# Two groups of a gated feed-forward as seven half-size products

## The chip, the core and the metric

The program runs on one core of a Trainium2 chip. The metric is the device time of one execution in microseconds (us). The three timed runs of the kernel before gave 1691.04, 1692.81 and 1693.84 us, so the median is 1692.81 us.

The engines are named as in the profile: PE (TensorE, matrix products; PEld is its weight load), DVE (VectorE), ACT (ScalarE), POOL (GpSimd), SP (SyncE, which here issues the loads of weights). All work in fp32: a product is made of three passes over operands that are split into a high part in the PE's own format (fp32r) and the rest (low part).

## The reference, cut to what matters

A decoder block of two layers is followed by a second block. The part that the change touches is that block's gated feed-forward: 512 tokens, model width 1024, inner width 2816.

```python
h = rmsnorm(x, g_ffn[i])
gate = causal_dwconv3(h @ w_gate[i], ffn_conv_w[i], ffn_conv_b[i])
x = x + (jax.nn.silu(gate) * (h @ w_up[i])) @ w_down[i]
```

`causal_dwconv3` adds to each token, per inner channel, weighted values of the two tokens before it. The gate's product and its partner's product (`h @ w_up`) have the same left operand.

## The kernel before

The normed tokens stand turned (features on partitions) as eight pairs of high and low parts, `xth` and `xtl`, 128 features by 512 tokens each. The inner width is cut into eleven groups (`gr`) of 256 channels. Each group has a part for the gate (`gp` in the profile) and one for the partner (`up`). `pair_of` loads the group's weights in two chunks of four feature blocks by 256 channels (`wr`, L170, 512 KB each). `split` makes the high part on ACT (`wh`, L119) and the low part on DVE (`wl`, L120). `mm3` issues three matmuls (L202 to L204) for each feature block and each half of the channels, with the weights stationary and all 512 tokens moving. So a part is 48 matmuls of 512 columns and a group is 96, accumulated in two PSUM banks per part.

`gate_ev` turns the gate's banks into `y`: a scaled copy on ACT (L1321), two DVE instructions for the convolution (L1322, L1324), then the silu on ACT (L1593). `up_ev` multiplies `y` by the partner's bank on DVE into `hr` (L1603). Group 0 is `gated_first`: its weights are there ahead, and it works on halves of 256 tokens, so that it can start when two of the four token tiles are normed and turned (`rms_norm`, L488 to L490, and `put_t`, L447). Groups 1 to 3 follow, then two rounds of `down_steps`. A round multiplies 1024 inner channels by `w_down` as seven products of half size: DVE makes sums of weight quarters (`wq`, L924) and of `hr` quarters (L915), `split` makes their parts (`wl`, `aop`), PE multiplies into banks `r`, and L885 adds them into `x`. Between the products of a round stand the parts of groups 4 to 10.

The order of the instructions on each engine is set at build time by a scheduler that takes the program's order and priorities (`high_priority`), and is fixed then; each engine works through its own list in order. Tiles come from pools: a new tile in a full pool waits until the old tile in its place has been read for the last time. The pool `wp` holds four pairs of `wh` and `wl`. The pool `fb` with the quarters of `w_down` opens after group 3 and takes memory that earlier pools have given back.

Of the kernel before, what the change touches and what calls it, by code (L numbers as in the profile page):

```python
# [12 lines left out]
F32 = mybir.dt.float32  # L13
F32R = mybir.dt.float32r
AF = mybir.ActivationFunctionType
ALU = mybir.AluOpType
AX = mybir.AxisListType

P = 128
# [7 lines left out]
W_PRIO = 60  # L27
# [17 lines left out]

WEAVE = (-1, -1, -1, 0, -1, 1, -1, -1, 2, -1, 3)
A_PRIO, B_PRIO = 120, 80
MLA_WO_AT = (0, 0, 21, 23)


@with_exitstack
def tile_hybrid_decoder(ctx: ExitStack, tc: tile.TileContext, io: dict, out: bass.AP):
    nc = tc.nc

    cst = ctx.enter_context(tc.tile_pool(name="cst", bufs=1))
    wp = ctx.enter_context(tc.tile_pool(name="wp", bufs=4))
# [6 lines left out]
    def pool(name, bufs, side=None):  # L63
        return tc.tile_pool(name=name, bufs=bufs, side=side, reuse_waits="tile")

    n_big = [0]

    def big(name, dt=F32R):
        n_big[0] += 1
        return bp.tile([P, 4, S], dt, tag="b", name=f"{name}_{n_big[0]}")  # L70

    def bank(name="pb"):
        n_big[0] += 1
        return ps.tile([P, S], F32, tag="ps", name=f"{name}_{n_big[0]}")
# [24 lines left out]
    def tick(n=1):  # L99

        clock[0] += 1
        while n and later and later[0][0] < clock[0]:
            later.popleft()[2]()
            n -= 1
# [13 lines left out]
    def split(hi, lo, src, src2=None):  # L118
        turned["hi"] = nc.scalar.copy(out=hi, in_=src).ins  # L119
        return nc.vector.tensor_tensor(out=lo, in0=src, in1=hi.bitcast(F32), op=ALU.subtract)  # L120
# [79 lines left out]
    def mm3(o, st, mv, start, stop):  # L200
        (sh, sl), (mh, ml) = st, mv
        nc.tensor.matmul(o, lhsT=sh, rhs=mh, start=start, stop=False, skip_group_check=True)  # L202
        nc.tensor.matmul(o, lhsT=sh, rhs=ml, start=False, stop=False, skip_group_check=True)  # L203
        nc.tensor.matmul(o, lhsT=sl, rhs=mh, start=False, stop=stop, skip_group_check=True)  # L204
# [43 lines left out]
    def krows(W, k0, kn, c0, n):  # L248
        return W[k0 * P:(k0 + kn) * P, c0:c0 + n].rearrange("(k p) c -> p k c", p=P)
# [316 lines left out]
    xt = new_xt()  # L566
# [22 lines left out]
    with ExitStack() as mla:  # L589
# [14 lines left out]
        def tmp(name):  # L604
            n_big[0] += 1
            return m4.tile([P, S], F32, tag="s", name=f"{name}_{n_big[0]}")
# [84 lines left out]
        for k in range(3):  # L691
            wh, wl = wchunk([(lambda raw: raw[:, :512].rearrange("p (h d) -> p h d", h=8),
                              w_uq[k * P:(k + 1) * P, :, 128:192])], 1, 512)
            rch.append((k, 1, wh, wl))
        for t in range(NB):
# [3 lines left out]
            a, b = tmp("ra"), tmp("rb")  # L699
# [3 lines left out]
            with tc.issue_after(turned["c"]):  # L703
                nc.vector.tensor_tensor(out=av, in0=pv, in1=rope[:, 0, t:t + 1, :].to_broadcast([P, 8, 64]),
                                        op=ALU.mult)
                nc.vector.tensor_tensor(out=bv, in0=pv, in1=rope[:, 1, t:t + 1, :].to_broadcast([P, 8, 64]),
                                        op=ALU.mult)
# [8 lines left out]
        PT, U = {}, {}  # L716
# [55 lines left out]
        for u in range(8 * NB + LAG + 1):  # L772
            h, qb = divmod(u, NB)
# [117 lines left out]
    ts2 = slice(0, 256), slice(256, 512)  # L891
# [185 lines left out]
    g, b = load_gb("ln_mix_g", "ln_mix_b", 0)  # L1077
    xt = new_xt()
# [67 lines left out]
    with swa:  # L1146
# [5 lines left out]
        PT, U, PO = {}, {}, {}  # L1152
# [162 lines left out]
    xt = new_xt()  # L1315
# [244 lines left out]
    xt = new_xt()  # L1560
# [11 lines left out]
    with pool("ff", 2) as ff:  # L1572
# [15 lines left out]
        def gate_ev(gr, banks):  # L1588
            for m in range(2):
                n_big[0] += 1  # L1590
                Y[gr, m] = y = ff.tile([P, S], F32, tag="y", name=f"y_{n_big[0]}")
                conv3(y, banks[m], V_FW, 22, gr * 2 + m, V_FB)
                nc.scalar.activation(y, y, AF.Silu)  # L1593

        def up_ev(gr, banks):
            if gr < 8 and gr % 2 == 0:
                RAW[gr // 2] = big("hr", F32)
            elif gr % 2 == 0:
                hh, hl = big("ah"), big("al")
                H.extend((hh[:, m, :], hl[:, m, :]) for m in range(4 if gr < 10 else 2))  # L1600
            for m in range(2):
                if gr < 8:
                    turned["y", gr] = nc.vector.tensor_tensor(  # L1603
                        out=RAW[gr // 2][:, gr % 2 * 2 + m, :], in0=Y.pop((gr, m)), in1=banks[m], op=ALU.mult).ins
                    continue
                n_big[0] += 1
                a = ff.tile([P, S], F32, tag="a", name=f"a_{n_big[0]}")
                nc.vector.tensor_tensor(out=a, in0=Y.pop((gr, m)), in1=banks[m], op=ALU.mult)
                split(*H[gr * 2 + m - 16], a)

        def gated(gr, part):

            banks = [bank("gu"[part] + "p") for _ in range(2)]
            pair_of(gr, (wg, wu)[part], banks)
            (gate_ev, up_ev)[part](gr, banks)

        def gated_first():
            banks = [bank("gt") for _ in range(2)] + [bank("up") for _ in range(2)]
            for hf in range(2):
                need(("xt", 2 * hf), ("xt", 2 * hf + 1))  # L1620
                for m in range(4):
                    half_m(banks[m], ahead.chunks[m], X, hf)
                    if hf == 0 and m < 2:
                        need(("xt", 2 + m))
            ahead.done()
            gate_ev(0, banks[:2])
            up_ev(0, banks[2:])
# [22 lines left out]
                to_ple(t)  # L1650

        gated_first()
        for gr in range(1, 4):
            for part in range(2):
                gated(gr, part)
        with pool("fb", 4) as fb:
# [108 lines left out]
```

## Time and profile before

| | |
|---|---|
| timed, median of 3 (range) | 1692.81 us (1691.04 to 1693.84) |
| the profiled execution | 1690.43 us, of which the profile spans 1688.6 us |
| busy: PE, DVE, ACT | 99%, 66%, 49% of the span |
| granted TensorE clock | 1.00 over the span |
| group 0 to the start of group 1 | 1270.81 to 1296.64 us |
| groups 1 to 3 | 1296.64 to 1361.94 us |

A matmul's time in the profile is from its start to its result, and the next one starts before that. What a matmul costs in a row of matmuls is therefore the distance between two starts. For DVE and ACT the time of one instruction is nearly what it costs.

### The profile page before, as it was taken

How to read it: one execution, taken by the hardware profiler on the slowest of the kernel's cores; microseconds unless marked ns; L12 is line 12 of the kernel's file. 1: busy time of each engine (PE TensorE's matmuls, PEld its weight loads, DVE VectorE, ACT ScalarE, POOL GpSimd, SP SyncE). 2: the span in 40 equal slices, each digit the busy share in tenths (PEclk: the TensorE clock that was granted, in tenths of full speed). 3: DMA queues.
4: the chain of work that ended last, by engine and by line, in shares of the span. 5: the costliest groups of instructions: out<-in, count | busy, mean ns of one | idle time of the engine just before them, and what ended most of it. 6: DMA issues, size and time to landing. Idle time of an engine off the chain costs nothing.

```text
span 1688.6 us, 21336 instructions
## 1 busy us (share of the span) xinstructions
PE 1669.5 (99%) x8239; PEld 1384.7 (82%) x8239; DVE 1111.0 (66%) x1938; ACT 829.3 (49%) x1416; POOL 25.6 (2%) x43
## 2 busy tenths in 40 slices
PE   8999999999999999999999999999999999999998
PEld 8777898888888877798888888988779888888887
DVE  5876648576846578738586846556765567577463
ACT  4665445444543578445444545444854343344442
POOL 0000000000001110000000000001000000000000
PEclk9999999999999999999999999999999999999999
DMA  5213244333132323413333143133352323422321
GB/s 181 69 46 130 88 150 119 100 100 100 50 125 87 101 63 119 156 50 101 101 99 100 50 126 111 39 125 99 100 187 63 88 76 99 125 63 63 113 88 63
DMA packets 125015, 165.22 MB, mean 98 GB/s; under 512 B 9385, under 2 KB 80322, under 8 KB 124914
## 3 DMA queue, kind: packets, MB, share of 16 engines
q1 hardware_dynamic: 119072, 150.03, 28.2%
q10 hardware_dynamic: 4626, 10.94, 1.9%
q0 software_dynamic: 1216, 2.89, 0.8%
q8 instruction: 65, 1.06, 0.3%
q14 instruction: 36, 0.29, 0.1%
HBM read 160.95 MB, written 2.88 MB: 97 GB/s over the span
## 4 chain that ended last, share of the span: by engine, by line
PE 94%; DVE 3%; ACT 1%; DMA 1%; issue 0%; SPq 0%; ACTq 0%; DVEq 0%
PE up L202 8%; PE up L204 8%; PE up L203 8%; PE r L202 6%; PE r L204 6%; PE r L203 6%; PE tt L203 3%; PE tt L204 3%; PE tt L202 3%; PE tm L202 2%; PE tm L203 2%; PE fm L202 2%; PE tm L204 2%; PE fm L203 2%; PE fm L204 2%; PE gp L204 2%
## 5 line engine op out<-in xcount | busy, mean ns | idle before, releaser
L120 DVE TENSOR_TENSOR wl<-wr,wh 128x1024 fp32r<-128x1024 f32 (+5 forms) x219 | 222.8, 1032 | 168.8 <-ACT wh L119 167.7
L119 ACT CAST wh<-wr 128x1024 fp32r<-128x1024 f32 (+5 forms) x219 | 193.6, 898 | 273.1 <-PE up L203 118.0
L202 PE MATMUL up<-xth,wh 128*128 128x512 f32 x608 | 236.5, 389 | 0.0
L203 PE MATMUL up<-xtl,wh 128*128 128x512 f32 x608 | 236.5, 389 | 0.0
L204 PE MATMUL up<-xth,wl 128*128 128x512 f32 x608 | 236.5, 389 | 0.0
L120 DVE TENSOR_TENSOR wl<-wq,wh 128x1024 fp32r<-128x1024 f32 x112 | 136.4, 1223 | 101.0 <-ACT wh L119 100.9
L119 ACT CAST wh<-wq 128x1024 fp32r<-128x1024 f32 x112 | 118.0, 1054 | 159.2 <-PE r L204 82.4
L204 PE MATMUL r<-wh,aop 128*128 128x512 f32 x448 | 174.3, 389 | 0.0
L202 PE MATMUL r<-wh,aop 128*128 128x512 f32 x448 | 174.3, 389 | 0.0
L203 PE MATMUL r<-wl,aop 128*128 128x512 f32 x448 | 174.3, 389 | 0.0
L204 PEld LDWEIGHTS up<-xth,wl 128*128 128x128 f32 x608 | 114.1, 188 | 23.8
L203 PEld LDWEIGHTS up<-xtl,wh 128*128 128x128 f32 x608 | 114.1, 188 | 23.6
L202 PEld LDWEIGHTS up<-xth,wh 128*128 128x128 f32 x608 | 114.1, 188 | 23.5
L204 PEld LDWEIGHTS r<-wh,aop 128*128 128x128 f32 x448 | 84.1, 188 | 17.5
L203 PEld LDWEIGHTS r<-wl,aop 128*128 128x128 f32 x448 | 84.1, 188 | 17.4
L202 PEld LDWEIGHTS r<-wh,aop 128*128 128x128 f32 x448 | 84.1, 188 | 17.4
L885 DVE SCALAR_TENSOR_TENSOR x<-x,r 128x512 f32<-128x512 f32 x144 | 92.5, 684 | 5.4 <-PE r L204 5.4
L120 DVE TENSOR_TENSOR aop<-hr,aop 128x1024 fp32r<-128x1024 f32 x56 | 67.0, 1221 | 21.5 <-ACT aop L119 21.5
L924 DVE TENSOR_TENSOR wq<-wq,wq 128x1024 f32<-128x1024 f32 x64 | 76.2, 1223 | 6.4 <-DMA wq<-in_w_down_dram 3.9
L202 PE MATMUL gp<-xth,wh 128*128 128x512 f32 x160 | 62.3, 389 | 0.0
L203 PE MATMUL gp<-xtl,wh 128*128 128x512 f32 x160 | 62.3, 389 | 0.0
L204 PE MATMUL gp<-xth,wl 128*128 128x512 f32 x160 | 62.2, 389 | 0.0
(426 smaller groups left out, 3561.4 us busy)
## 6 DMA issues: line engine op xcount, KB each, us to landing
wr<-in_mlp_w_up_dram SPq DMA_DIRECT2D x64, 512.0 KB, 3.8
wq<-in_mlp_w_down_dram SPq DMA_DIRECT2D x48, 512.0 KB, 4.3
wr<-in_w_in_dram SPq DMA_DIRECT2D x24, 512.0 KB, 3.6
wr<-in_w_gate_dram SPq DMA_DIRECT2D x22, 512.0 KB, 3.7
wr<-in_w_up_dram SPq DMA_DIRECT2D x22, 512.0 KB, 3.6
wr<-in_mlp_w_down_dram SPq DMA_DIRECT2D x16, 512.0 KB
wq<-in_w_down_dram SPq DMA_DIRECT2D x16, 512.0 KB, 7.8
wr<-in_mla_w_o_dram SPq DMA_DIRECT2D x8, 512.0 KB, 3.7
```

What stands on the lines that cost most here:

```text
L119: turned["hi"] = nc.scalar.copy(out=hi, in_=src).ins
L120: return nc.vector.tensor_tensor(out=lo, in0=src, in1=hi.bitcast(F32), op=ALU.subtract)
L202: nc.tensor.matmul(o, lhsT=sh, rhs=mh, start=start, stop=False, skip_group_check=True)
L203: nc.tensor.matmul(o, lhsT=sh, rhs=ml, start=False, stop=False, skip_group_check=True)
L204: nc.tensor.matmul(o, lhsT=sl, rhs=mh, start=False, stop=stop, skip_group_check=True)
L885: nc.vector.scalar_tensor_tensor(out=x[:, t, cs], in0=x[:, t, cs], scalar=alpha, in1=pb, op0=ALU.mult, op1=ALU.add)
L924: nc.vector.tensor_tensor(out=out[:, ks, :], in0=a[:, ks, :], in1=b[:, ks, :], op=op)
```

## The change

`SEVEN = 4` makes groups 2 and 3 take a new way; group 1 keeps the old one. For such a group the product of the tokens (two halves of 256 tokens, two halves of 512 features) and of the weights (two halves of 512 features, gate or partner) is made from seven products of half size instead of eight. `x_operands` makes four sums of token quarters once and splits them (`xr`, `xs`). `gated_seven` loads four quarters (`fq`), makes four sums of them in place (L1657), splits seven operands (`wh`, `wl`), and multiplies in seven steps of 24 matmuls with 256 tokens moving, into three banks (named `gt`). The banks are added up into the gate `fg` and the partner `fu` in SBUF, with `fp` (the first product) and `fv` between them (L1678). `gate_ev` and `up_ev` then work from SBUF.

```diff
+SEVEN = 4
...
+        def x_operands():
+
+            raw = [big("xr", F32) for _ in range(2)]
+            for i in range(2):
+                for th in (0, 1):
+                    nc.vector.tensor_tensor(out=raw[i][:, :, ts2[th]], in0=xt[0][i][:, :, ts2[th]].bitcast(F32),
+                                            in1=xt[1][i][:, :, ts2[th]].bitcast(F32), op=ALU.add)
+            A11, A21, A12, A22 = [raw[i][:, :, ts2[th]] for i in range(2) for th in range(2)]
+
+            def op(out, a, b, how):
+                nc.vector.tensor_tensor(out=out, in0=a, in1=b, op=how)
+                o = big("xs").rearrange("p k c -> p (k c)").rearrange("p (f k c) -> p f k c", f=2, k=4)
+                split(o[:, 0], o[:, 1], out)
+                return o[:, 0], o[:, 1]
...
+            ops["s3"] = op(A21, A11, A21, ALU.subtract)
+            ops["s2"] = op(A22, A22, A21, ALU.subtract)
+            ops["s1"] = op(A11, A11, A22, ALU.add)
+            ops["s4"] = op(A12, A12, A22, ALU.subtract)
+            return ops
+
+        def gated_seven(gr, fm, ops):
+
+            B = {}
+            for r in range(2):
+                for h, W in enumerate((wg, wu)):
+                    n_big[0] += 1
+                    B[r, h] = q = fm.tile([P, 4, 256], F32, tag="q", name=f"fq_{n_big[0]}", bufs=4)
+                    nc.sync.dma_start(out=q, in_=krows(W, 4 * r, 4, gr * 256, 256))
+            B11, B12, B21, B22 = B[0, 0], B[0, 1], B[1, 0], B[1, 1]
...
+            def b_sum(out, a, b, how):
+                with tc.high_priority(offset=W_PRIO):
+                    nc.vector.tensor_tensor(out=out, in0=a, in1=b, op=how)
+
+            def product(R, B, a, start):
+                n_big[0] += 1
+                wh = wp.tile([P, 1024], F32R, tag="wh", name=f"wh_{n_big[0]}")
+                wl = wp.tile([P, 1024], F32R, tag="wl", name=f"wl_{n_big[0]}")
+                with tc.high_priority(offset=W_PRIO):
+                    split(wh, wl, B.rearrange("p k c -> p (k c)"))
+                wh, wl = (t.rearrange("p (k c) -> p k c", k=4) for t in (wh, wl))
+                ah, al = ops[a]
+                for m in range(2):
+                    for k in range(4):
+                        cs = slice(m * P, (m + 1) * P)
+                        mm3(R[:, m * 256:m * 256 + 256], (wh[:, k, cs], wl[:, k, cs]), (ah[:, k, :], al[:, k, :]),
+                            start and m == 0 and k == 0, k == 3)
+                tick()
...
+            def plus(out, a, R):
+                nc.vector.tensor_tensor(out=out, in0=a, in1=both(R), op=ALU.add)
+
+            G, U = tmp("g", 2), tmp("u", 2)
+            p1, v = tmp("p"), tmp("v")
+            R1, R2, R3 = bank("gt"), bank("gt"), bank("gt")
+            product(R1, B11, "a11", True)
+            nc.scalar.copy(out=p1, in_=both(R1))
+            b_sum(B12, B22, B12, ALU.subtract)
+            product(R3, B12, "s3", True)
+            plus(v, p1, R3)
+            b_sum(B11, B12, B11, ALU.add)
+            product(R2, B11, "s2", True)
+            plus(G[:, :, ts2[1]], p1, R2)
+            product(R1, B21, "a12", False)
+            nc.scalar.copy(out=G[:, :, ts2[0]], in_=both(R1))
+            b_sum(B21, B21, B11, ALU.subtract)
+            product(R3, B21, "a22", False)
+            plus(G[:, :, ts2[1]], G[:, :, ts2[1]], R3)
+            gate_ev(gr, [G[:, m, :] for m in range(2)])
+            b_sum(B11, B22, B11, ALU.subtract)
+            product(R2, B11, "s1", False)
+            plus(U[:, :, ts2[1]], v, R2)
+            product(R2, B22, "s4", False)
+            plus(U[:, :, ts2[0]], p1, R2)
+            up_ev(gr, [U[:, m, :] for m in range(2)])
...
-        for gr in range(1, 4):
+        ops = x_operands()
+        gated(1, 0)
+        gated(1, 1)
+        with pool("fm", 1) as fm:
+            for gr in range(2, SEVEN):
+                gated_seven(gr, fm, ops)
+        for gr in range(SEVEN, 4):
             for part in range(2):
                 gated(gr, part)
```

Line numbers of the changed kernel are one higher than before from L46 on. First place: DVE in the norm ahead of group 0, where `rr`, `ra` and `ro` are small steps of the reciprocal root for a token tile, `x1` is the residual that takes a bank `tt`, and `xn` the normed tile. Before:

```order
L423 RECIPROCAL rr_1649_11168<-rv_1648_11167 128x1
L426 SCALAR_TENSOR_TENSOR ra_1651_11170<-rv_1648_11167,rs_1650_11169 128x1
L430 SCALAR_TENSOR_TENSOR ro_1652_11171<-ra_1651_11170,rs_1650_11169 128x1
L490 SCALAR_TENSOR_TENSOR xn_1646_11164<-x1_375_1792,ro_1652_11171,row_1640_11131 128x1024
L1512 SCALAR_TENSOR_TENSOR x1_375_1792<-tt_1654_11192,rsa_9109,x1_375_1792 128x512
```

Now:

```order
L424 RECIPROCAL rr_1649_11168<-rv_1648_11167 128x1
L1657 TENSOR_TENSOR fq_1707_11692<-fq_1709_11696,fq_1707_11692 128x1024
L427 SCALAR_TENSOR_TENSOR ra_1651_11170<-rv_1648_11167,rs_1650_11169 128x1
L1513 SCALAR_TENSOR_TENSOR x1_375_1792<-tt_1654_11192,rsa_9109,x1_375_1792 128x512
L431 SCALAR_TENSOR_TENSOR ro_1652_11171<-ra_1651_11170,rs_1650_11169 128x1
L491 SCALAR_TENSOR_TENSOR xn_1646_11164<-x1_375_1792,ro_1652_11171,row_1640_11131 128x1024
```

The first sum of weight quarters stands inside the norm, and the residual's addition of the next bank has come ahead of `xn`. In the same way it has come ahead of the next tile's `xn`.

Second place: DVE at the end of group 3, from its gate's convolution to the low part of the first weights of the first down round (`wl_1752`; in the program before that row is `wl_1726`). Before:

```order
L120 TENSOR_TENSOR wl_1726_11957<-wq_1721_11941,wh_1726_11956 128x1024
L924 TENSOR_TENSOR wq_1721_11941<-wq_1723_11947,wq_1721_11941 128x1024
L1322 SCALAR_TENSOR_TENSOR y_1715_11864<-gp_1711_11802,vec_78,y_1715_11864 128x511
L1324 SCALAR_TENSOR_TENSOR y_1715_11864<-gp_1711_11802,vec_78,y_1715_11864 128x510
L120 TENSOR_TENSOR wl_1727_11961<-wq_1721_11941,wh_1727_11960 128x1024
```

Now:

```order
L1323 SCALAR_TENSOR_TENSOR y_1743_12088<-fg_1731_11933,vec_78,y_1743_12088 128x511
L1323 SCALAR_TENSOR_TENSOR y_1744_12093<-fg_1731_11933,vec_78,y_1744_12093 128x511
L1325 SCALAR_TENSOR_TENSOR y_1743_12088<-fg_1731_11933,vec_78,y_1743_12088 128x510
L1325 SCALAR_TENSOR_TENSOR y_1744_12093<-fg_1731_11933,vec_78,y_1744_12093 128x510
L1678 TENSOR_TENSOR fu_1732_11934<-fv_1734_11936,gt_1736_11938 128x2x256
L1678 TENSOR_TENSOR fu_1732_11934<-fp_1733_11935,gt_1736_11938 128x2x256
L1604 TENSOR_TENSOR hr_1726_11922<-y_1743_12088,fu_1732_11934 128x512
L1604 TENSOR_TENSOR hr_1726_11922<-y_1744_12093,fu_1732_11934 128x512
L121 TENSOR_TENSOR aop_1767_12330<-hr_1726_11922,aop_1767_12330 128x1024
L916 TENSOR_TENSOR hr_1726_11922<-hr_1726_11922,hr_1689_11526 128x4x256
L916 TENSOR_TENSOR hr_1689_11526<-hr_1689_11526,hr_1726_11922 128x4x256
L121 TENSOR_TENSOR wl_1752_12179<-wq_1747_12163,wh_1752_12178 128x1024
```

The first down weights stood ahead of group 3's convolution; now they stand behind everything that group 3 leaves to do, behind a split of a quarter of `hr` and behind two sums of `hr` quarters.

Third place: PE where group 2 ends (`gt_1715`, its seventh product) and group 3 has begun (`gt_1737`, its second product):

```order
L205 MATMUL gt_1737_11939<-xs_1692_11536,wl_1739_11971 128x256
L203 MATMUL gt_1737_11939<-xs_1692_11536,wh_1739_11970 128x256
L203 MATMUL gt_1715_11703<-xs_1695_11548,wh_1725_11893 128x256
L204 MATMUL gt_1715_11703<-xs_1695_11548,wh_1725_11893 128x256
```

Group 3's first product and 13 matmuls of its second stand ahead of group 2's seventh. At the end of group 3 nothing stands between its sixth product, its seventh and the first down product (`r_1754`).

## Rows read from the trace of the kernel before

**Rows 1.** The page: busy share of the engines; the chain that ended last, by engine.
```profile
PE 1669.5 (99%) x8239; PEld 1384.7 (82%) x8239; DVE 1111.0 (66%) x1938; ACT 829.3 (49%) x1416; POOL 25.6 (2%) x43
PE 94%; DVE 3%; ACT 1%; DMA 1%; issue 0%; SPq 0%; ACTq 0%; DVEq 0%
```
**Rows 2.** PE's waits: line, releaser, us in total, times, longest.
```profile
PE pt L447 <- DMA x<-in_x_dram: 6.6, 2, 4.7
PE pt L754 <- ACT pr L498: 1.3, 1, 1.3
```
**Rows 3.** Stretches: length, busy us (count) of PE, PEld, DVE, ACT, POOL, clock, DMA.
```profile
1296.50:1361.90 65.40, 65.40 (x291) 54.19 (x290) 34.09 (x36) 21.20 (x25) 0.00 (x0) 1.00 0.25 71
1361.90:1480.00 118.10, 118.10 (x522) 97.79 (x522) 82.26 (x88) 46.95 (x51) 0.00 (x0) 1.00 0.35 104
```
**Rows 4.** Timeline of PE (start, us): group 0's second half, groups 1 and 2 beginning.
```profile
1285.12 0.28 PE L202 MATMUL gt<-xth,awh 128*128 128x256 f32 x1
1296.64 0.40 PE L202 MATMUL gp<-xth,wh 128*128 128x512 f32 x1
1318.42 0.39 PE L202 MATMUL gp<-xth,wh 128*128 128x512 f32 x1
```
**Rows 5.** Groups by line and shape, 1296.5 to 1400 us (count | busy, mean ns).
```profile
L119 ACT CAST aop<-hr 128x1024 fp32r<-128x1024 f32 x7 | 7.1, 1049 | 0.7 <-DVE hr L915 0.7
L120 DVE TENSOR_TENSOR aop<-hr,aop 128x1024 fp32r<-128x1024 f32 x6 | 7.1, 1219 | 0.0
L1321 ACT ACTIVATE y<-gp,vec 128x512 f32<-128x512 f32 x8 | 6.2, 775 | 7.5 <-PE gp L204 7.5
L1603 DVE TENSOR_TENSOR hr<-y,up 128x512 f32<-128x512 f32 x9 | 6.2, 685 | 7.8 <-PE up L204 7.8
L1322 DVE SCALAR_TENSOR_TENSOR y<-gp,vec,y 128x511 f32<-128x511 f32 x8 | 6.0, 749 | 6.2 <-ACT y L1321 6.2
L924 DVE TENSOR_TENSOR wq<-wq,wq 128x1024 f32<-128x1024 f32 x4 | 4.9, 1220 | 0.0
```
**Rows 6.** Timeline of DVE: the norm's second and third steps ahead of group 0.
```profile
1264.16 0.16 DVE L423 RECIPROCAL rr<-rv 128x1 f32<-128x1 f32 x1
1264.59 0.22 DVE L426 SCALAR_TENSOR_TENSOR ra<-rv,rs 128x1 f32<-128x1 f32 x1 [0.27 <-ACT rs L424]
1265.04 1.28 DVE L490 SCALAR_TENSOR_TENSOR xn<-x,ro,row 128x1024 f32<-128x1024 f32 x1
1266.24 0.75 DVE L1512 SCALAR_TENSOR_TENSOR x<-tt,rsa,x 128x512 f32<-128x512 f32 x1
...
1268.02 1.28 DVE L490 SCALAR_TENSOR_TENSOR xn<-x,ro,row 128x1024 f32<-128x1024 f32 x1
```
**Rows 7.** Timeline of PE: the transposes of these tiles, and group 0 beginning.
```profile
1268.56 1.91 PE L447 MATMUL pt<-ident,xn 128*128 128x128 f32 x16
1270.81 0.38 PE L202 MATMUL gt<-xth,awh 128*128 128x256 f32 x1 [0.34 <-ACT xth L119]
```
**Rows 8.** Timeline of ACT, DVE and PE: first down weights, first down product.
```profile
1345.60 1.05 ACT L119 CAST wh<-wq 128x1024 fp32r<-128x1024 f32 x1 [4.38 <-PE gp L203]
1346.68 1.23 DVE L120 TENSOR_TENSOR wl<-wq,wh 128x1024 fp32r<-128x1024 f32 x1 [4.21 <-ACT wh L119]
1361.72 0.39 PE L204 MATMUL up<-xth,wl 128*128 128x512 f32 x1
1361.94 0.39 PE L202 MATMUL r<-wh,aop 128*128 128x512 f32 x1
```
**Rows 9.** Loads of the down weights: timeline of SP; the page's row.
```profile
1253.15 4.20 SPq L902 DMA_DIRECT2D wq<-in_w_down_dram  x8
wq<-in_w_down_dram SPq DMA_DIRECT2D x16, 512.0 KB, 7.8
```
**Rows 10.** Timeline of PE: eight transposes after the first wait, and eight later.
```profile
4.75 1.94 PE L447 MATMUL pt<-ident,x 128*128 128x128 f32 x8 [4.75 <-DMA x<-in_x_dram]
1278.50 1.04 PE L447 MATMUL pt<-ident,xn 128*128 128x128 f32 x8
```

More of the change, by code (lines that the diff above doesn't have):

```diff
@@ L1615, in gated @@
             (gate_ev, up_ev)[part](gr, banks)
+        def x_operands():
[10 more added lines that the diff above has]
+                return o[:, 0], o[:, 1]
+            q = {i + 1: (xt[0][i // 2][:, :, ts2[i % 2]], xt[1][i // 2][:, :, ts2[i % 2]]) for i in range(4)}
+            ops = {"a11": q[1], "a12": q[3], "a22": q[4]}
+            ops["s3"] = op(A21, A11, A21, ALU.subtract)
[3 more added lines that the diff above has]
+            return ops
@@ new lines, in gated_seven, with tmp, both @@
+        def gated_seven(gr, fm, ops):
[6 more added lines that the diff above has]
+            B11, B12, B21, B22 = B[0, 0], B[0, 1], B[1, 0], B[1, 1]
+            def tmp(name, w=1):
+                n_big[0] += 1
+                return fm.tile([P, 2, 256 * w], F32, tag=name, name=f"f{name}_{n_big[0]}")
+            def b_sum(out, a, b, how):
+                with tc.high_priority(offset=W_PRIO):
+                    nc.vector.tensor_tensor(out=out, in0=a, in1=b, op=how)
+            def product(R, B, a, start):
+                n_big[0] += 1
+                wh = wp.tile([P, 1024], F32R, tag="wh", name=f"wh_{n_big[0]}")
[10 more added lines that the diff above has]
+                tick()
+            def both(R):
+                return R.rearrange("p (m c) -> p m c", m=2)
+            def plus(out, a, R):
[23 more added lines that the diff above has]
+            up_ev(gr, [U[:, m, :] for m in range(2)])
```

## The prediction

> **What bounds the kernel now.** I read the page's shares first, then the chain of waits, then the places where PE waits. PE is busy 99% of the span and holds 94% of the chain that ended last [rows 1]. Its longest wait after the first loads is 1.3 us [rows 2]. So a microsecond of PE work taken out, with nothing put in its way, is a microsecond of the program, and a microsecond that PE is made to wait is one lost. Groups 1 to 3 are pure PE time: 65.4 of 65.4 us, while DVE is busy 34.1 and ACT 21.2 [rows 3]. What the reader should see there is that the change trades the full engine against one that is half empty, and that the trade is good as long as DVE's list never stands in front of PE.
>
> The profiled execution took 1690.4 us, of which 1688.6 are the span. The timed median is 2.4 us above it. I make the sum against the profiled execution and add it to the median.
>
> **PE's own work.** A matmul of 512 columns costs the distance of two starts: group 1's 96 take 1318.42 - 1296.64 = 21.78 us, 0.227 each. The last 96 of 256 columns in group 0 take 1296.64 - 1285.12 = 11.52 us, 0.120 each [rows 4]. So half the columns cost 53%, not 50%. A seven-product group is 7 x 24 x 0.120 = 20.16 us instead of 21.78: **1.6 us less per group, 3.2 for two**. The eighth part that Strassen's scheme saves (2.7) loses 1.1 to the shorter matmuls.
>
> The Trainium skill's page "TensorE: Matmul & The Clock Gate" (Back-to-back issue gap) gives 518 cycles for 512 columns and 262 for 256, an estimate of 0.216 and 0.109 us at 2.4 GHz. By it the saving would be 2 x (96 x 0.216 - 168 x 0.109) = 4.8 us. The trace has both distances for this very pattern of weights, and I stay with 3.2.
>
> **What DVE gets.** A pass over 1024 elements is 1.22 us, over 512 elements 0.69, a convolution step 0.75; ACT's cast of 1024 is 1.05 and its scaled copy 0.78 [rows 5]. Added are 12 passes in `x_operands`, and per group three more splits, four sums and five additions: 12 x 1.22 + 2 x (7 x 1.22 + 5 x 0.69) = 38.6 us. The four sums of down weights (L924) fall behind the stretch, -4.9. DVE then has 34.1 + 38.6 - 4.9 = 67.8 us of work where PE has 65.4 - 3.2 = 62.2. Most of it is hidden at first: ahead of the first product's weights DVE has some 15 us of list from the end of group 0 on, and group 1 gives PE 21.8. The weights of the next products follow with about as much lead. But the lead is eaten, and DVE is full when group 3 ends.
>
> **Where PE waits.** Four places, in order of time.
>
> (a) The norm ahead of group 0. The first weight sum (1.22) stands between `rr` and `ra`, where DVE idled only 0.27, and the residual's addition now stands ahead of `xn` twice. Walked along the list [rows 6]: the weight sum ends at 1265.5; the addition waits for its bank until 1266.0 and ends at 1266.7; `xn` ends at about 1268.2, the next one, behind a further addition, at about 1271.4 instead of 1269.3. PE covers little of it: the first eight of the sixteen transposes end near 1269.5, and group 0 waits for the rest [rows 7]. Ends: 1.22 - 0.27 = 0.95, if the additions cost nothing, and 2.1 - 0.2 = 1.9. I take **1.5**, the middle, since both rows stand equally near.
>
> (b) Group 2's seventh product adds into the bank of the sixth, which DVE must read first, and that reading stands behind the gate's convolution. From the fifth product's end: 0.16 to the result, addition 0.69, scaled copy 0.78, four steps 3.0, addition 0.69 = 5.3 us, with a sum and a split of the next group between them 7.8. PE has its sixth product (2.88), group 3's first (2.88) and 13 matmuls (1.56) meanwhile, 7.3. **0.5**, between 0 and 1.7 (another pass in front).
>
> (c) Group 3's seventh product has the same chain and no cover but the sixth: 5.3 - 2.9 = 2.4, up to 3.7 if a pass of 1.22 has just begun when the fifth product ends (the split of an `hr` quarter stands there). I take **2.8**, nearer the lower end, since that pass will be part done.
>
> (d) The junction with the down round. Before, the first down weights were split at 1345.60 and 1346.68, 15 us before their product began 0.22 us behind group 3's last matmul [rows 8]. Now they stand last. After the seventh product: 0.16 to the result; one addition into `fu` and two products into `hr`, 3 x 0.69; ACT's cast of the quarter, 1.05; then on DVE its low part, two sums of quarters and the weights' low part, 4 x 1.22. Together 0.16 + 2.07 + 1.05 + 4.88 = 8.2 us, in which PE runs only two matmuls that need the high part alone (0.45). **7.7**, between 7.2 (passes that follow each other closely may save 0.1 each) and 8.2.
>
> Behind it I count nothing more. The four moved weight sums (4.9) fall into a stretch where DVE is busy 82.3 of 118.1 us [rows 3]. Nothing is given back either: PE is full there.
>
> The loads: the eight of the first down round were issued together at 1253.15 and landed in 7.8 us at the median [rows 9]. In the changed order they wait for memory of group 3: the first quarter until its last weights are split, about 12 us before it is needed, the others until `fu` and `hr` are read, 11 us (the junction's DVE list and the next passes) before DVE sums them. 7.8 hides in both, by 3 to 4 us.
>
> **Sum.** -3.2 + 1.5 + 0.5 + 2.8 + 7.7 = **+9.3 us**: 1699.7 for an execution like the profiled one, 1702.1 beside the median. The low ends give -3.2 + 0.95 + 0 + 2.4 + 7.2 = +7.4, the high ones -3.2 + 1.9 + 1.7 + 3.7 + 8.2 = +12.3, so 1700.2 to 1705.1 for this case. A change under 0.2% (3.4 us) could not be told from none here.
>
> **Rivals.** *The clock falls at the junction.* PE would stand still some 2.8 us, work 2.9, then wait 7.7 with two matmuls in it. No wait of this length occurs once the program runs, and the granted clock reads 1.00 (2.4 GHz) in both stretches [rows 3]. But after its first wait, of 4.75 us, eight transposes took 1.94 us, and 1.04 later on [rows 10]: nearly double. A second set of that kind and a few matmuls more would make 2 to 2.5 us lost. Price: +9.3 + 2.3 = 1704.4. The page named above says in its Part 1 that an array which has idled is put back to 1.2 GHz and must work for a while to regain 2.4; by that rule the junction would pay this. The trace agrees [rows 10], and no row shows what an idle stretch in the midst of the program does. Chance 0.24.
>
> *The down weights land late.* The margin is 3 to 4 us. If landing took 12 us instead of 7.8, DVE would stand at the first weight sum and with it the splits behind. Price 1 to 4 us beyond the forecast, 1704.6. Against it: before, eight loads stood in the queue at once too. Chance 0.07.
>
> *The half-size matmuls issue at exactly half.* 336 x (0.120 - 0.1134) = 2.2 us less: 1699.9. The starts speak against it [rows 4]. Chance 0.05.
>
> *Not slower: the element passes run at twice the speed.* The place is DVE in (a) to (d), where nearly all operands are in SBUF. With every DVE pass halved, (a) is 0.5, (b) 0, (c) 0.3 (0.16 + 0.35 + 0.78 + 1.5 + 0.35 - 2.88) and (d) 0.16 + 1.03 + 1.05 + 2.44 - 0.45 = 4.2; the sum is +1.8, 1694.6, and it is not slower from about 0.75 us per pass of 1024 on. For it speaks only that the additions in `fg` and `fu` occur nowhere before; against it L924, whose operands are in SBUF too, at 1.22 [rows 5]. Chance 0.04, and 0.02 that it is faster still.
>
> **How the numbers follow.** The forecast has 0.58. Cases with more than +3.4 us hold 0.58 + 0.24 + 0.07 + 0.05 = 0.94, less 0.01 for their tails: slower 0.93; the halved passes give same 0.05 and faster 0.02. The range reaches from a little below the forecast's low end and the exact half to above the clock's price: 1698.8 to 1706.2.
>
> **What would show it.** In the changed profile: products of 24 matmuls, 2.88 us apart at the first starts where PE doesn't wait; the second tile's transposes and group 0 some 1.5 us late; a PE wait for DVE's `fu` of about 2.8 us ahead of group 3's seventh product; a wait of `r` on L203 for `wh` of about 4 us and on L204 for `wl` of 3 to 4 right behind it; the granted clock there. Wrong would be: no wait of `r` over 2 us; the waits on a load instead of DVE and ACT; or a lost stretch behind the junction, in groups 4 to 10, of more than a microsecond.

## The result, and the profile after

The changed kernel took 1705.7 us (median of four, 1703.8 to 1706.9) beside 1693.1 us for the kernel before in the same runs: a ratio of 1.0075, 95% interval 1.0058 to 1.0093, so 10 to 16 us slower. In a second set it took 1705.5 us, ratio 1.0083 (1.0069 to 1.0097). The forecast was 1702.1, the rival with the falling clock 1704.4. The profiled execution took 1706.7 us with a span of 1704.9, 16.3 longer than before's.

The page's shares and its chain hardly differ from before [rows 1]; PE has 92% of the chain instead of 94%, and DVE is busy 67% of the span instead of 66%:

```profile
PE 1673.9 (98%) x8383; PEld 1394.1 (82%) x8383; DVE 1145.5 (67%) x1974; ACT 841.8 (49%) x1430; POOL 25.7 (2%) x43
```

The loss shows in PE's waits between 1262 and 1405 us, where the longest of before was 0.6 us. Columns as there: line, releaser, us in total, times, longest.

```profile
PE r L203 <- ACT wh L120: 4.2, 1, 4.2
PE r L204 <- DVE wl L121: 2.7, 1, 2.7
PE gt L203 <- ACT y L1594: 2.3, 1, 2.3
PE gt L203 <- DVE fu L1678: 1.7, 1, 1.7
PE pt L448 <- DVE xn L491: 1.5, 1, 1.5
...
PE gt L205 <- DVE wl L121: 0.3, 1, 0.3
...
```

The five long ones are the forecast places: the norm (`pt`), both seventh products (`gt`), the junction (`r`). The third row names ACT's `y`, but `y` feeds no product; the seventh product adds into a bank that DVE's `fu` must read first, and `fu` ended 0.14 us before the product began (DVE's 1362.73 + 0.68 below). With a bank of its own (e2) the wait is gone. A releaser is the event that came last by the profile, not always the operand.

With two short ones of group 0 (0.3 and 0.2) the waits sum to 13.2 us, and those of before in the same window to 0.9; with 3.2 saved that leaves 9.1 of 16.3. The rest stands in PE's own rows. Timeline of PE after: start, duration (us).

```profile
1319.81 0.28 PE L203 MATMUL gt<-xth,wh 128*128 128x256 f32 x1
1322.68 0.28 PE L203 MATMUL gt<-xs,wh 128*128 128x256 f32 x1
...
1341.96 0.28 PE L203 MATMUL gt<-xs,wh 128*128 128x256 f32 x1
1343.91 0.58 PE L203 MATMUL gt<-xs,wh 128*128 128x256 f32 x1 [1.67 <-DVE fu L1678]
1344.29 0.41 PE L204 MATMUL gt<-xs,wh 128*128 128x256 f32 x1
1344.50 0.41 PE L205 MATMUL gt<-xs,wl 128*128 128x256 f32 x1
...
1347.04 0.28 PE L205 MATMUL gt<-xs,wl 128*128 128x256 f32 x1
...
1360.96 0.28 PE L205 MATMUL gt<-xs,wl 128*128 128x256 f32 x1
1363.55 0.36 PE L203 MATMUL gt<-xs,wh 128*128 128x256 f32 x1 [2.32 <-ACT y L1594]
...
1367.87 0.28 PE L205 MATMUL gt<-xs,wl 128*128 128x256 f32 x1
1372.35 1.22 PE L203 MATMUL r<-wh,aop 128*128 128x512 f32 x2 [4.20 <-ACT wh L120]
1376.32 0.79 PE L204 MATMUL r<-wl,aop 128*128 128x512 f32 x1 [2.75 <-DVE wl L121]
...
1379.47 0.63 PE L203 MATMUL r<-wh,aop 128*128 128x512 f32 x1
1379.89 0.63 PE L204 MATMUL r<-wl,aop 128*128 128x512 f32 x1
...
1383.69 0.39 PE L203 MATMUL gp<-xth,wh 128*128 128x512 f32 x1
```

Read the distance of starts. The first product takes 1322.68 - 1319.81 = 2.87 us for 24 matmuls, 0.120 each, as forecast. Behind the first long wait the starts stand 0.21 apart, until 1347.04; behind the second the same from 1364.11 on, half a microsecond after PE had begun again; and the `r` matmuls 0.42 apart instead of 0.227, until about 1381. In these stretches the granted clock is 0.50, the lower level of 1.2 GHz; elsewhere it is 1.00. Windows of after (columns as in [rows 3]):

```profile
1319.80:1340.00 20.20, 20.20 (x170) 20.19 (x169) 14.99 (x15) 8.47 (x10) 0.00 (x0) 1.00 0.30 88
1344.00:1347.00 3.00, 3.00 (x14) 3.00 (x15) 2.97 (x3) 0.00 (x0) 0.00 (x0) 0.50 0.00 0
1364.00:1367.50 3.50, 3.50 (x19) 3.50 (x18) 0.00 (x0) 0.00 (x0) 0.00 (x0) 0.51 0.00 0
1376.30:1381.00 4.70, 4.68 (x11) 3.72 (x12) 4.70 (x5) 1.48 (x2) 0.00 (x0) 0.50 0.67 228
1383.70:1480.00 96.30, 96.30 (x426) 79.76 (x425) 67.58 (x72) 37.56 (x41) 0.00 (x0) 1.00 0.36 109
```

A window full of PE is no proof of full pace: three of these five are full, or nearly, at half speed. The last row answers to the second of [rows 3]: behind the junction PE is full again and nothing is lost.

The stretch from group 2's first matmul to the end of the span gives a measure that variations ahead of it don't touch: 1688.6 - 1318.42 = 370.2 us before, 1704.9 - 1319.81 = 385.1 after. Of its +14.9, and of the start that comes 1319.81 - 1318.42 = 1.4 later, this is the account, all from the starts above and those between them: PE's work -3.2; around group 2's seventh product +2.4 of waiting (0.6 ahead of it, around 1340.67, where group 3's second product waits for its low weights, and at the product itself 1343.91 - 1341.96 - 0.12) and +1.45 at half pace (14 distances, 3.13 - 14 x 0.120); at group 3's +2.5 (1363.55 - 1360.96 - 0.12) and +1.5 (17 distances, 3.54 - 17 x 0.120); at the junction +7.9 (the third `r` matmul at 1376.32 instead of 1367.87 + 0.12 + 2 x 0.227) and +2.4 (7.37 us for the other 22 matmuls, less 22 x 0.227). Together 14.95. The clock is 5.35 of it.

DVE's list shows why the waits are there (after; the norm, then group 2's last part, then the junction):

```profile
1264.30 0.16 DVE L424 RECIPROCAL rr<-rv 128x1 f32<-128x1 f32 x1
1264.38 1.23 DVE L1657 TENSOR_TENSOR fq<-fq,fq 128x1024 f32<-128x1024 f32 x1
...
1269.88 1.28 DVE L491 SCALAR_TENSOR_TENSOR xn<-x,ro,row 128x1024 f32<-128x1024 f32 x1
...
1336.52 1.23 DVE L1657 TENSOR_TENSOR fq<-fq,fq 128x1024 f32<-128x1024 f32 x1 [2.77 <-DMA fq<-in_w_up_dram]
...
1362.73 0.68 DVE L1678 TENSOR_TENSOR fu<-fv,gt 128x512 f32<-128x512 f32 x1
1368.18 0.69 DVE L1678 TENSOR_TENSOR fu<-fp,gt 128x512 f32<-128x512 f32 x1 [4.78 <-PE gt L205]
1368.97 1.29 DVE L1604 TENSOR_TENSOR hr<-y,fu 128x512 f32<-128x512 f32 x2
1371.38 1.23 DVE L121 TENSOR_TENSOR aop<-hr,aop 128x1024 fp32r<-128x1024 f32 x1 [1.11 <-ACT aop L120]
1372.64 2.48 DVE L916 TENSOR_TENSOR hr<-hr,hr 128x1024 f32<-128x1024 f32 x2
1375.04 1.22 DVE L121 TENSOR_TENSOR wl<-wq,wh 128x1024 fp32r<-128x1024 f32 x1
```

The norm is as walked: the sum `fq` stands right behind `rr`, and the `xn` that started at 1268.02 before [rows 6] starts at 1269.88. What it costs PE is read between two fixed matmuls: the first `wo` ahead of the norm, which waits for ACT in every run, and group 2's first. First `wo` of before, then of after:

```profile
1253.90 0.50 PE L202 MATMUL wo<-wh,yah 128*128 128x512 f32 x1 [0.81 <-ACT yah L123]
```
```profile
1254.00 0.50 PE L203 MATMUL wo<-wh,yah 128*128 128x512 f32 x1 [0.79 <-ACT yah L124]
```

That is 1318.42 - 1253.90 = 64.52 us before and 1319.81 - 1254.00 = 65.81 after, so 1.3 us for the norm; 0.1 of the 1.4 lies ahead of it. Seven other kernels with this norm have 65.79 to 65.82. The junction too: `wl`, which PE needs at once, is last behind `fu`, `hr`, `aop` and two sums. The row at 1336.52 was not forecast: DVE stood idle 2.77 us for group 3's fourth quarter of weights, and that idle time came just ahead of what frees group 2's seventh product.

### The profile page after: what moved, and what is told of

The parts are those of the page before. It is cut to its first block, busy times and chain, and to the rows that moved or that the text cites. A ratio compares the mean times of both kernels' runs of the same rounds, so it can differ in the third digit from the quotient of the medians.

```text
span 1704.9 us, 21692 instructions
## 1 busy us (share of the span) xinstructions
PE 1673.9 (98%) x8383; PEld 1394.1 (82%) x8383; DVE 1145.5 (67%) x1974; ACT 841.8 (49%) x1430; POOL 25.7 (2%) x43
## 4 chain that ended last, share of the span: by engine, by line
PE 92%; DVE 4%; ACT 1%; DMA 1%; issue 1%; SPq 0%; ACTq 0%; DVEq 0%
PE up L205 8%; PE up L203 8%; PE up L204 8%; PE r L204 6%; PE r L205 6%; PE r L203 6%; PE tt L204 3%; PE tt L205 3%; PE tt L203 3%; PE tm L203 2%; PE tm L204 2%; PE tm L205 2%; PE fm L203 2%; PE fm L205 2%; PE fm L204 2%; PE gp L203 2%
## 5 line engine op out<-in xcount | busy, mean ns | idle before, releaser
L121 DVE TENSOR_TENSOR wl<-wr,wh 128x1024 fp32r<-128x1024 f32 (+5 forms) x211 | 213.0, 1025 | 154.9 <-ACT wh L120 153.8
L120 ACT CAST wh<-wr 128x1024 fp32r<-128x1024 f32 (+5 forms) x211 | 185.2, 892 | 249.8 <-PE up L204 103.4
L204 PE MATMUL up<-xtl,wh 128*128 128x512 f32 x576 | 224.1, 389 | 0.0
L205 PE MATMUL up<-xth,wl 128*128 128x512 f32 x576 | 224.1, 389 | 0.0
L203 PE MATMUL up<-xth,wh 128*128 128x512 f32 x576 | 224.1, 389 | 0.0
L204 PEld LDWEIGHTS up<-xtl,wh 128*128 128x128 f32 x576 | 108.1, 188 | 22.5
L205 PEld LDWEIGHTS up<-xth,wl 128*128 128x128 f32 x576 | 108.1, 188 | 22.5
L120 ACT CAST aop<-hr 128x1024 fp32r<-128x1024 f32 x56 | 57.2, 1047 | 12.5 <-DVE hr L1604 6.8
L203 PE MATMUL fm<-xth,wh 128*128 128x256 f32 (+1 forms) x192 | 61.4, 320 | 0.2 <-ACT xth L120 0.2
L204 PE MATMUL fm<-xtl,wh 128*128 128x256 f32 (+1 forms) x192 | 61.0, 318 | 0.0
```

## The experiments

Theory 1: the loss is PE waiting at these places for entries that stand late in DVE's and ACT's lists, and the clock that falls in or behind those waits. The main rival: DVE's load itself is the bound, and the waits only show it. The last column is the stretch from group 2's first matmul to the end, in the profiled execution, less the 370.2 of before; it leaves out the norm's 1.3. Two profiles of the changed kernel differ by 2.4 us in it (after and e5), because the clock fell three times in one and twice in the other and group 2's wait was shorter in e5; so a smaller difference between two profiles does not by itself show what an edit is worth.

| kernel | median, us | ratio to before (95%) | stretch, us |
|---|---|---|---|
| changed | 1705.7 | 1.0075 (1.0058 to 1.0093) | +14.9 |
| e5 changed, again | 1705.5 | 1.0083 (1.0069 to 1.0097) | +12.5 |
| e1 down early | 1698.0 | 1.0041 (1.0029 to 1.0054) | +5.0 |
| e2 own bank | 1701.2 | 1.0056 (1.0042 to 1.0070) | +8.1 |
| e3 one group | 1691.3 | 1.0001 (0.9992 to 1.0010) | -1.4 |
| e4 filler | 1702.6 | 1.0065 (1.0053 to 1.0078) | +10.0 |
| e6 norm | 1700.6 | 1.0053 (1.0040 to 1.0065) | +9.1 |
| e7 all four | 1687.8 | 0.9978 (0.9969 to 0.9987) | -3.2 |
| e8 one group, tuned | 1689.5 | 0.9988 (0.9979 to 0.9996) | -1.5 |
| e9 junction only | 1692.6 | 1.0008 (0.9999 to 1.0016) | -0.7 |
| e10 quarters early | 1704.2 | 1.0082 (1.0069 to 1.0094) | +11.0 |
| e11 gate later | 1703.2 | 1.0067 (1.0055 to 1.0079) | +10.6 |

Before took 1691.4, 1691.1 and 1691.4 us beside e1 to e4, e5 to e8 and e9 to e11.

**e1, the first down weights early.**

```diff
-        b = b_op(B11)
+        b = [wchunk(krows(wd, row + 2 * i, 2, 0, 512), 2, 512) for i in range(2)] if first else b_op(B11)
```

> The first down product's weights come through the ordinary weight buffers as well (two more loads of 0.5 MB), so that their splits no longer stand behind group 3's last results in the lists of VectorE and ScalarE. Theory 1 (the junction waits because those two splits are queued late): the waits of 4.2 and 2.7 us before the first r go, with the 2.4 us that the r product loses at the low clock; but the third down product, whose weights still land in memory that group 3 frees late, then waits some 4 us of its own. In all 5 to 7 us off: about 1699.5. Theory 2 (the junction waits for group 3's results, its gates times partners and the sums made of them): nothing changes, 1705 to 1706.

It came out at 1698.0, 7.4 us off against e5 and a little more than expected, and both waits before the first `r` are gone; so the place of two splits in two lists was the wait, not group 3's results. The gain is not the junction's alone: as in e9 below, 17 of the first down product's 24 matmuls now stand ahead of group 3's seventh product, whose wait is gone with them. What is given back is there too, at the second down product (the expectation calls it the third), with a clock of 0.53 behind it (timeline of PE, then a window):

```profile
1381.08 0.73 PE L203 MATMUL r<-wh,aop 128*128 128x512 f32 x2 [2.11 <-ACT wh L120]
1383.20 0.79 PE L204 MATMUL r<-wl,aop 128*128 128x512 f32 x1 [1.39 <-DVE wl L121]
```
```profile
1382.00:1388.00 6.00, 4.80 (x11) 3.79 (x12) 6.00 (x7) 2.94 (x3) 0.00 (x0) 0.53 0.03 4
```

**e2, a bank of its own.**

```diff
-            product(R2, B22, "s4", False)
             plus(U[:, :, ts2[0]], p1, R2)
+            R4 = bank("gt")
+            product(R4, B22, "s4", True)
+            plus(U[:, :, ts2[0]], U[:, :, ts2[0]], R4)
```

> The seventh product of each group gets a bank of its own and is added by one more VectorE pass a group, so it no longer waits until VectorE has read the sixth's. Theory 1 (the seventh product is late because its bank is read behind other entries of VectorE's list, and the clock falls in that wait): the waits of 1.7 and 2.3 us go, and the 1.2 and about 1.5 us lost at the low clock behind them; the junction gets some 1.5 us of it back as a longer wait, so 4 to 5 us off: about 1701. Theory 2 (VectorE's load in groups 2 and 3 is the bound, and the wait only shows it): two passes of 0.6 us more, so 0 to 1.5 us slower, 1706 to 1707.

1701.2: both waits and the half pace behind them went, with two passes more on DVE. The rival of DVE's load would have made it slower. The first wait of `r` grew from 4.2 to 5.9 us, as said.

**e3, one group.**

```diff
-SEVEN = 4
+SEVEN = 3
```

> Group 2 alone goes by seven products, group 3 as before. Theory 1: the norm chain (+1.4) and a wait at group 2's seventh product of 0.5 us stay (there is no quarter of a group 3 to wait for), too short a wait for the clock to fall; the PE gains 1.6; the junction behind an ordinary group waits for nothing. About as long as before: 1693 to 1694.5. Theory 2 (each group by seven products costs about the same, half of the 12.7 us): 1699.

1691.3, no different from before, and some 2 to 3 us under what was expected: the wait of 0.5 us at group 2's seventh product did not occur, and the norm's 1.3 and the PE's 1.6 nearly cancel. One group costs nothing net and two cost 12.7 to 14.3: the price is not per group. It comes with the second one: its late quarter, its end, and the junction behind it.

**e4, filler.** Results of the added matmuls are not used.

```diff
+                for i in range(fill):
+                    nc.tensor.matmul(R1[:, 0:256], lhsT=wh[:, i % 4, 0:P], rhs=ah[:, i % 4, :],
+                                     start=i == 0, stop=i == fill - 1, skip_group_check=True)
...
+                for i in range(30):
+                    turned["fill"] = nc.tensor.matmul(R1[:, :], lhsT=X[0][0][:, 0:P], rhs=X[i % 8][0],
+                                                      start=i == 0, stop=i == 29, skip_group_check=True).ins
```

> Matmuls whose results nothing uses stand where the PE waits: 14 and 18 of 256 columns before the seventh products of groups 2 and 3 (1.7 and 2.2 us), 30 of 512 columns before the first down product (6.8 us). Nothing that the PE waits for comes earlier by it. Theory 1 (the waits let the clock fall, and the half pace behind them costs about 5 us in all): the three stretches at half pace go to full pace, and less what the filler overshoots 3.5 to 5 us come off: about 1701.5. Theory 2 (the half pace has another cause, such as the loads that run at that time): 1706 to 1707, the rows still at 0.213 and 0.43 us.

More work for PE, and the time fell by 2.9 us against e5 (1705.5), the stretch by 4.9 and 2.4 against the two profiles of the changed kernel. That is less than expected; at group 2 the filler left 1.1 us of wait. The clock reads 1.00 where it had read 0.50:

```profile
1344.00:1348.00 4.00, 3.69 (x30) 3.69 (x31) 1.91 (x3) 1.33 (x2) 0.00 (x0) 1.00 0.00 0
1366.00:1374.00 8.00, 8.00 (x41) 6.67 (x39) 5.66 (x7) 3.23 (x4) 0.00 (x0) 1.00 0.60 212
1374.00:1382.00 8.00, 7.10 (x32) 5.64 (x31) 8.00 (x8) 3.71 (x4) 0.00 (x0) 1.00 0.77 263
```

The loads that ran in the last two of these windows did not slow it. The half pace is a result of the waits.

**e5, the changed kernel again.**

> The changed kernel itself, to have it on the chip of the next three. Both theories: 11.5 to 13 us above before, with the waits at the same places; the clock's part may vary from run to run by 1 to 2 us.

14.3 us above before, a little more than expected. Group 2's wait was 1.51 us this time, and the clock did not fall behind it; at group 3 and at the junction it fell as in the first profile (timeline of PE, then windows):

```profile
1347.25 0.39 PE L203 MATMUL gt<-xs,wh 128*128 128x256 f32 x1 [1.51 <-DVE fu L1678]
```
```profile
1347.00:1351.00 4.00, 3.75 (x31) 3.75 (x32) 3.97 (x5) 0.51 (x2) 0.00 (x0) 1.00 0.00 0
1366.00:1368.00 2.00, 2.00 (x11) 2.00 (x11) 0.00 (x0) 0.00 (x0) 0.00 (x0) 0.50 0.00 0
```

**e6, the norm.** The sums of group 2 are queued behind group 0's partners.

```diff
+                    if gr == 2:
+                        es.enter_context(tc.issue_after(turned["y", 0]))
```

> The three sums of weight quarters of group 2 are held back on VectorE until group 0's partners are done; nothing else is changed. Theory 1 (the first sum, queued between the last scores' addition and the norm, makes the transposes late, and on both sides of it group 3's chain sits a little late on VectorE): the wait before the transposes falls from 1.5 to 0.1 us or less, and the wait at group 3's seventh product by 1 to 2 us; 2 to 3.5 us off: about 1702.5. Theory 2 (the chain behind the norm is covered by group 0's own waits for its operands, so the delay is given back there): under 0.7 us off.

1700.6, 4.8 off against e5, more than expected. In the profiles 1.2 of it is at the norm (64.57 us between the two matmuls instead of 65.79), and 3.4 in the stretch, because group 3's wait fell to 0.87 us and the clock stayed up there (1.00 in 1358 to 1366). A sum moved at 1264 us changed the order of DVE's list 90 us later: `fu` now stands between the steps of group 3's convolution. So e6 is no test of the norm alone.

**e7, all four edits.** e6's edit with those shown at e9, e10 and e11:

```diff
+        for r, h in ((1, 1), (0, 1), (0, 0), (1, 0)) if first else B:
...
+                        es.enter_context(tc.issue_after(turned["y", 0]))
...
+                B[r, h] = q = fm.tile([P, 4, 256], F32, tag="q", name=f"fq_{n_big[0]}", bufs=5)
...
+            gate_ev(gr, [G[:, m, :] for m in range(2)])
```

> Four edits to the changed kernel together: the first down product's weights through the ordinary buffers, with the down loads issued in the order in which they are wanted; group 3's quarters through a fifth buffer, so that they land earlier; the gates' convolution put behind the partners' first sum on VectorE; the sums of quarters held back until the norm is done. Theory 1 (the loss is these waits and the clock behind them, and nothing else): all go, and the 3.2 us of PE work that the change saves come through: 2 to 3.5 us under before, 1688 to 1690. Theory 2 (VectorE's load in groups 2 and 3, or a wait that none of the edits reaches, takes their place): 1 to 5 us above before.

1687.8, 3.4 us under before and the fastest of all. The stretch is 3.2 us shorter, the forecast's PE term. Windows:

```profile
1318.00:1340.00 22.00, 22.00 (x176) 21.57 (x175) 20.53 (x23) 11.57 (x13) 0.00 (x0) 1.00 0.25 72
1340.00:1362.00 22.00, 22.00 (x179) 21.61 (x179) 20.99 (x24) 13.34 (x16) 0.00 (x0) 1.00 0.17 49
1362.00:1386.00 24.00, 24.00 (x109) 19.89 (x108) 22.68 (x26) 11.25 (x12) 0.00 (x0) 1.00 0.81 274
```

DVE is busy 64.2 of 68 us and PE never waits. The program has the 1974 DVE instructions of the changed kernel. So DVE's load was not the bound; the order of its list and the times of a few loads were.

**e8, one group tuned.** With e6's edit and e11's:

```diff
-SEVEN = 4
+SEVEN = 3
```

> Group 2 alone by seven products, with the sums of quarters held back and the gates' convolution put behind the partners' first sum. Theory 1: the norm chain is as before and no wait is left, so the 1.6 us that the PE saves in one group come through: 1.0 to 1.8 us under before. Theory 2 (half-size products cost more than their rows show, or the wait moves): within 0.7 us of before.

1689.5, 1.7 under before: one group's 1.6.

**e9, the junction alone.**

```diff
+        for r, h in ((1, 1), (0, 1), (0, 0), (1, 0)) if first else B:
...
-        b = b_op(B11)
+        b = [wchunk(krows(wd, row + 2 * i, 2, 0, 512), 2, 512) for i in range(2)] if first else b_op(B11)
```

> Of the four edits of the kernel with all four only the one at the junction: the first down product's weights through the ordinary buffers, and the down loads issued in the order in which they are wanted; the norm chain, the quarters and the order of VectorE's list in the groups stay as in the changed kernel. Theory 1 (the junction alone is the largest part: 4.2 + 2.7 us of waits and 2.4 us at half pace, with 1 us of wait left at the third down product): 8.5 to 11 us off the changed kernel's 1705.5, so 1694.5 to 1697. Theory 2 (the junction only collects what the groups before it run late): 3 to 6 us off.

12.9 off against e5, more than expected; its median is 1.2 above before's, which the interval (0.9999 to 1.0016) does not tell from no difference. The reason stands in PE's order. With its weights out of the way of group 3's list, 17 of the first down product's 24 matmuls stand between group 3's sixth and seventh products, so they cover that wait as well (timeline of PE):

```profile
1359.78 0.28 PE L205 MATMUL gt<-xs,wl 128*128 128x256 f32 x1
1359.90 0.40 PE L203 MATMUL r<-wh,aop 128*128 128x512 f32 x1
...
1363.78 0.39 PE L203 MATMUL r<-wh,aop 128*128 128x512 f32 x1
1364.01 0.28 PE L203 MATMUL gt<-xs,wh 128*128 128x256 f32 x1
```

**e10, the quarters early.**

```diff
-            for r in range(2):
-                for h, W in enumerate((wg, wu)):
...
+            for r, h in (((0, 1), (1, 0), (0, 0), (1, 1)), ((0, 0), (1, 1), (0, 1), (1, 0)))[gr - 2]:
...
+                B[r, h] = q = fm.tile([P, 4, 256], F32, tag="q", name=f"fq_{n_big[0]}", bufs=5)
```

> Only the loads of the weight quarters: a fifth buffer, and the quarters asked for in the order in which buffers come free and sums want them, so that group 3's fourth quarter is there when VectorE reaches its sum. Theory 1 (that load, on which VectorE sat idle for 2.0 to 2.8 us, is what makes the wait before group 2's seventh product long enough for the clock to fall): VectorE's idle goes, that wait falls from 1.5 to 1.7 us to under 0.5, the clock stays up there (1.2 us), and group 3's wait shrinks a little: 2 to 3.5 us off, about 1702.5. Theory 2 (VectorE has slack there, and the idle time costs nothing): under 0.7 us off.

In the trace as theory 1 had it: DVE's sum now starts without a wait, and group 2's wait is gone from the list.

```profile
1335.41 1.22 DVE L1656 TENSOR_TENSOR fq<-fq,fq 128x1024 f32<-128x1024 f32 x1
```

In time it is short of it: 1.2 us against e5 by the medians, and by the ratios (1.0082 and 1.0083) nothing that could be told. In the stretch it is 1.5 us against e5, where only the wait and no fall of the clock was to be won at this place, and 3.9 against the first profile. That the wait comes from this load is shown; what it is worth in time is not settled.

**e11, the gate later.**

```diff
-            gate_ev(gr, [G[:, m, :] for m in range(2)])
             b_sum(B11, B22, B11, ALU.subtract)
             product(R2, B11, "s1", False)
             plus(U[:, :, ts2[1]], v, R2)
+            gate_ev(gr, [G[:, m, :] for m in range(2)])
```

> Only the order of VectorE's list: the gates' convolution (four passes of 0.7 us a group) is put behind the partners' first sum, so that the sixth product's bank is read earlier. No pass is added or left out. Theory 1 (the seventh product waits for that sum's place in the list, not for VectorE's load): group 2's wait falls from 1.6 to under 0.6 us and group 3's from 2.4 to under 1.9, and the clock does not fall behind group 2's: 2 to 4 us off, about 1702.5. Theory 2 (the load is the bound, so a later convolution makes the products that follow late by as much): within 0.7 us of the changed kernel.

1703.2, 2.3 off against e5, without a pass less on DVE. Group 2's wait stayed at 1.50, against the expectation, because DVE's idle time for the late quarter (2.04 us here) lies ahead of it; group 3's fell from 2.4 to 0.99, and the clock did not fall behind either (1.00 in 1340 to 1348 and in 1358 to 1366):

```profile
1342.18 0.39 PE L203 MATMUL gt<-xs,wh 128*128 128x256 f32 x1 [1.50 <-DVE fu L1678]
...
1361.79 0.36 PE L203 MATMUL gt<-xs,wh 128*128 128x256 f32 x1 [0.99 <-DVE fu L1678]
```

## Why the prediction was right, and where it fell short

The direction, the mechanism of the waits and the four places were right; the number was 3.6 us low, and inside its range by 0.5. That it lies inside is in part luck. The forecast's own sum had the clock steady, and for the profiled execution it was 7.0 us short (+16.3 instead of +9.3): 5.35 are the clock and 1.9 the wait in (b). The upper end had room for one fall of the clock, where three came, and the second set's +14.3 would have lain beyond it (1706.2 is +13.4).

- **PE's own work, -3.2:** right. e7 leaves nothing but this term, and its stretch is 3.2 us shorter. The 4.8 that came of the Trainium skill's page "TensorE: Matmul & The Clock Gate" (Back-to-back issue gap) did not show; the measured distance of 0.120 decides.
- **(a) the norm, 1.5:** measured 1.3. Group 0 itself begins 1.75 late [rows 7] and gives part of it back in its own waits for `xth` and `xtl`.
- **(b) group 2's seventh product, 0.5:** this is the step that failed. The walk took the quarters of group 3 as landed. The fourth was asked for at 1330.90, when group 2 had let go of its buffer, and DVE stood 2.77 us for it. Measured 2.4: 1.8 at the product itself, just above the end of 1.7, and 0.6 at group 3's second product, a place that the walk had at nothing. With the quarters early (e10) both waits are gone. I had asked when the down weights land [rows 9] and not when these do.
- **(c) group 3's seventh product, 2.8:** measured 2.5.
- **(d) the junction, 7.7:** measured 7.9, the weights last in the list as walked. But DVE was not "full when group 3 ends": it stood idle 4.78 us for the seventh product right ahead of this chain, so the wait is the chain's length and not a backlog; the loads of the first down quarter were there (both `r` waits name ACT and DVE).
- **The rival of the clock (0.24):** it came true and was mis-sized. It priced one fall at the junction, 2.3; that one cost 2.4, but two more came behind the waits of 1.7 and 2.3 us, 1.45 and 1.5. The forecast's sum without any of them, with (b) as measured, would be -3.2 + 1.4 + 2.4 + 2.5 + 7.9 = +11.0 (with 1.4, the later start of group 2); with all three it is 16.3, and the timed runs, +12.7 and +14.3, lie between. By the Trainium skill's page "TensorE: Matmul & The Clock Gate" (Part 1) an idled array goes back to 1.2 GHz. The trace agrees, with a clock of 0.50 or 0.51 in three windows, but not behind every wait (1.00 behind the 1.51 us in e5). The slow transposes of [rows 10] carry less than the prediction gave them: the granted clock reads 1.00 over them too (4.75 to 6.70 us), so no run here shows that the clock made them slow.
- **The other rivals:** the down weights were not late; half the columns do not issue in half the time (0.120 against 0.227); the element passes are no faster (1.22 to 1.23 per 1024).
- **Behind the junction, nothing:** right (96.3 of 96.3 us).

Of the 12.7 to 14.3 us the junction and what hangs on it are by far the most: with e9's edit alone, which also covers group 3's seventh product, the kernel is within 1.2 us of before.

## What to carry to other kernels

When work is traded from a full engine to a half-empty one, ask not how much the other engine has to do but where in its list the entries stand that the full engine waits for: here the same 1974 DVE instructions made a kernel 14 us slower than before in one order and, with a few loads moved, 3 us faster in another. At each change of stage look for what the next stage needs first, and keep its loads, buffers and splits clear of the stage before. A wait on PE costs more than its length when the clock falls in or behind it, here 1.2 to 2.4 us each time.

## What the runs showed of the hardware

The clock's fall is not the same in each execution. It was at its lower level behind waits of 2.3 and 2.4 us and behind one of 1.67 us, and it stayed up behind waits of 1.51, 1.50, 1.30, 1.19 and 1.18 us at the same product as the 1.67. In e4 it fell ahead of group 0, behind the norm's wait of 1.49 us: from the first `wo` to group 2's first matmul it is 66.98 us there, 1.2 more than in the other kernels with that wait. In e5 it also fell far ahead of the change, where the waits were hardly other than in the first profile (2.1 us there in two waits, 1.3 in one); group 2 then began 4.1 us later than in that profile (1323.87 against 1319.81), where e2's, without such a fall, began 1.9 later (1321.75). The window of e5:

```profile
75.00:85.00 10.00, 9.22 (x31) 6.13 (x29) 6.68 (x17) 5.37 (x13) 0.00 (x0) 0.67 0.23 68
```

Single runs of one kernel stand 5 us apart here (1702.9 to 1708.3 in e5). A stretch between two fixed matmuls with no fall in it repeats far more closely: the one across the norm varied by 0.03 us over the eight kernels with the same norm and no fall there.
